# Two buffers in turn for the experts' scaled outputs, one buffer for the low part of their input

## The chip, the cores and the metric

The kernel runs on one core of a Trainium2 chip. The core has a matrix engine (TensorE, PE in the profile), a vector engine (DVE), a scalar engine (ACT), a general engine (POOL) and a queue engine (SP) that only issues transfers. Each engine runs its own instructions strictly in their order. Transfers between memory and the on-chip buffers run on 16 DMA engines, whichever engine issued them. The metric is the device time of one execution in microseconds, as the median of several runs.

## The reference

A trunk of two layers over 1024 tokens of width 1024, all in 32-bit floats. Each layer mixes the tokens (attention for one half of the width, a recurrent delta rule for the other), projects, and then sends every token to 2 of 32 experts. The change lies in the experts alone:

```python
def block_mlp(args):
    tok, e = args                      # up to 128 tokens of expert e
    xb = h_pad[tok]                    # gather, 128 x 1024
    hid = jax.nn.silu(xb @ w_gate[e]) * (xb @ w_up[e])     # 128 x 256
    return hid @ w_down[e]             # 128 x 1024
...
y = jax.ops.segment_sum(yb.reshape(R, D) * row_w[:, None], row_tok, num_segments=T + 1)
...
x = x + gt2 * hier_moe(...)
```

Each output row is scaled with the weight of its token for that expert, and by the gate `gt2`, before the two rows of a token are added.

## The kernel before

`layer` runs twice, once per layer. In each it runs `phase_a` (norm, input projection, attention, recurrence), `out_proj` (output projection and routing), and then `moe`, the stage of the experts. Nothing of the next layer starts before `moe` has written all rows, since the next norm reads them.

`moe` loops over 35 blocks of up to 128 tokens: the 32 experts and 3 blocks for rows beyond 128. The weights of a block come as two halves of 1 MB for gate and up (`w_gu`, `load_gu`, L1586) and 1 MB for down (`w_d`, `load_d`, L1589), issued on SP. Halves live in 5 slots (`self.raw`), so half n takes the slot of half n-5. Each half is split into a rounded part `w_hi` (ACT, L1594) and the rest `w_lo` (DVE, L1595), in 3 pairs of tiles (`self.parts`).

For a block e the steps are these:

- `gather(e)` (POOL, L1614): an indirect transfer fetches the rows of its tokens into `xg`, two tiles in turn.
- `prepare(e)`: 8 transposes on PE (L1622) into `xT_ps`, a rounded copy `xT_hi` on ACT (L1630), and the rest `xT_lo` on DVE (L1631).
- `up(e)`: 24 matmuls on PE, in threes: `xT_hi` with `w_hi` (L1646), `xT_lo` with `w_hi` (L1647), `xT_hi` with `w_lo` (L1648).
- `hidden(e)`: the activation, one step on ACT (L1636) and two on DVE (L1637, L1638), into `th`.
- `turned(e)`: two transposes of `th` on PE (L1666), copied to `hT` on ACT (L1667).
- `down(e)`: 4 matmuls on PE (L1687) into `y_ps`; the trace has two records for each.
- `scaled(e)`: DVE multiplies `y_ps` with the row weights and `gt2` into `yo` (L1673).
- `scatter(e)` (POOL, L1676): an indirect transfer writes the rows of `yo` to their places in `yd`.

The order on PE, ACT, DVE and POOL is fixed by the code (`in_order`). In turn e of the loop it is: up(e); the split of half 2e+3; turned(e-1); prepare(e+1); gather(e+3); hidden(e); down(e-1); scaled(e-1); scatter(e-1); the split of half 2e+4. So on DVE one turn reads: `w_lo` of half 2e+3, `xT_lo` of e+1, two steps of `th`, `yo` of e-1, `w_lo` of half 2e+4. The loads on SP, the routing of the extra rows (`route_overflow`, L1563 and L1564, in the first turns) and the rest of the kernel are put in order by a scheduler.

`yo` is one tile with one buffer (`tag="x", bufs=1` in the pool `tx`). The tile of block e+1 is the same memory, so its writer waits until the transfer of block e has read it. `xT_lo` has two buffers in the pool `xE`.

Of the kernel before, what the change touches and what calls it, by code (L numbers as in the profile page):

```python
# [10 lines left out]
F32 = mybir.dt.float32  # L11
F32R = mybir.dt.float32r
# [3 lines left out]
OP = mybir.AluOpType  # L16
# [4 lines left out]
T = 1024  # L21
D = 1024
# [30 lines left out]
class Trunk:  # L53
# [1546 lines left out]
    def moe(self, l, side, psum):  # L1600

        nc, tc = self.nc, self.tc
        with ExitStack() as s:
            xp, tx = s.enter_context(self.pool(name="xE", bufs=2, side=side)), self.tx
            gt2 = tx.tile([128, D], F32, name="gt2", tag="v2", bufs=1)
# [12 lines left out]
            def transposed(e):  # L1618
                x = xg[e % 2]
                pt = psum.tile([128, 8, 128], F32, name="xT_ps", tag="xT", bufs=1)  # L1620
                for k in range(NK):
                    nc.tensor.transpose(pt[:, k, :], x[:, 128 * k:128 * k + 128], self.ident)  # L1622
                return pt

            def prepare(e):

                pt = transposed(e)
                hi = tx.tile([128, 8, 128], F32R, name="xT_hi", tag="hl")
                lo = xp.tile([128, 8, 128], F32R, name="xT_lo", tag="xT_lo")
                nc.scalar.copy(hi, pt)  # L1630
                nc.vector.tensor_tensor(lo, pt, hi.bitcast(F32), op=OP.subtract)  # L1631
                return hi, lo
# [18 lines left out]
            def prepare_late(e):  # L1651
                pt = transposed(e)
                nc.scalar.copy(late, pt)
                return late
# [11 lines left out]
                    nc.tensor.transpose(pt[:, k, :], ths[:, e % 2, 128 * k:128 * k + 128], self.ident)  # L1666
                nc.scalar.copy(hT, pt)  # L1667

            yos = {}

            def scaled(e, po):
                yo = yos[e] = tx.tile([128, D], F32, name="yo", tag="x", bufs=1)
                nc.vector.scalar_tensor_tensor(yo, po, self.wsl[:, e:e + 1], gt2, op0=OP.mult, op1=OP.mult)  # L1673

            def scatter(e):
                st = nc.gpsimd.indirect_dma_start(out=self.yd, out_offset=bass.IndirectOffsetOnAxis(ap=self.idx_s[:, e:e + 1], axis=0),  # L1676
                                                  in_=yos.pop(e), in_offset=None, bounds_check=2 * T - 1, oob_is_err=False)
                for o in scat:
                    tc.declare_no_dep(st.ins, o.ins, reason="every slot holds another row")
                scat.append(st)  # L1680

            def down(e):
                w = self.wd[e % 3]
                po = psum.tile([128, D], F32, name="y_ps", tag="y", bufs=1)
                for half in range(2):
                    for k in range(2):
                        nc.tensor.matmul(po[:, 512 * half:512 * half + 512], hT[:, k, :], w[:, k, 512 * half:512 * half + 512],  # L1687
                                         start=(k == 0), stop=(k == 1))
                scaled(e, po)
# [16 lines left out]
            gather(0)  # L1706
            gather(1)
            x, last = prepare(0), {}
            gather(2)
            for e in range(N):  # L1710
                with self.in_order(last):
                    ph = up(e, x)
                    if e + 1 < N:
                        self.split_half(2 * e + 3)
                    if e:
                        turned(e - 1)
                    if e + 1 < N:
                        x = prepare(e + 1)
                    if e + 3 < N:
                        gather(e + 3)  # L1720
                    hidden(e, ph)
                if e == 0:
                    nc.sync.dma_start(gt2, self.mod_row(l, 5).partition_broadcast(128))
                with self.in_order(last):
                    if e:
                        down(e - 1)
                        scatter(e - 1)
                    if e + 2 < N:
                        self.split_half(2 * e + 4)
                for n in (2 * e + 8, 2 * e + 9):  # L1730
                    if n < 2 * N:
                        self.load_gu(l, n, expert(n // 2))
                if e and e + 2 < N:
                    self.load_d(l, e + 2, expert(e + 2))
                if e == 2:
                    self.route_overflow(xp, psum)
            turned(N - 1)
            down(N - 1)
            scatter(N - 1)
            late = self.lay.tile([128, 8, 128], F32, name="xT", tag="sg")  # L1740

            n = nc.values_load(self.ovf[0:1, 0:1], min_val=0, max_val=15)
            with ExitStack() as ifs:
                for b in range(self.MORE_E, 15):
                    ifs.enter_context(tc.If(n > b))
                    if b == self.MORE_E:
                        gather(32 + b)
                        overflow(b)
                    x = prepare_late(32 + b)
                    if b + 1 < 15:  # L1750
                        gather(33 + b)
                        overflow(b + 1)
                    up_late(32 + b, x)
                    turned(32 + b)
                    down(32 + b)
                    scatter(32 + b)
# [191 lines left out]
```

## Time and profile before

| | |
|---|---|
| median of 3 runs | 2877.4 us (2875.11 to 2880.29) |
| the profiled execution | 2878.6 us, of which the span from the first to the last instruction is 2876.6 us |
| PE busy | 2426.0 us, 84% of the span |
| DVE busy | 1862.8 us, 65% |
| ACT busy | 1108.6 us, 39% |
| POOL busy | 875.3 us, 30% |
| mean granted clock of PE | 0.904 of full speed |
| first to last copy of `hT`, layer 0 | 1038.2 to 1410.4 us |
| first to last copy of `hT`, layer 1 | 2430.4 to 2812.0 us |

The copy of `hT` (L1667) runs once per block at a fixed place in PE's order, so the distance of two such copies is the time of one block. The shares of busy time are means over stages with different limits; for a change in the experts the stretches 1038 to 1410 us and 2430 to 2812 us are to be read by themselves. A wait "<-X" is the idle time of an engine before an instruction, put down to what ended it.

### The profile page before, as it was taken

The numbers are of one execution on the slowest core, as the hardware profiler recorded it, in microseconds if no ns is written. First come the engines' busy times: TensorE is split into PE (matmuls) and PEld (weight loads), VectorE is DVE, ScalarE is ACT, GpSimd is POOL, SyncE is SP. The second block draws the span as 40 slices with busy tenths as digits, with TensorE's granted clock in tenths as the row PEclk, the third lists the DMA queues.
The fourth block names the chain that finished last, engine by engine and source line by source line (L and its number), as shares of the span: only waits on it lengthen the run. The fifth ranks groups of instructions, "written<-read, shape, count | busy, mean of one in ns | idle before, by whom it ended". The sixth has DMA issues, their size and how long they took to land.

```text
span 2876.6 us, 45429 instructions
## 1 busy us (share of the span) xinstructions
PE 2426.0 (84%) x17313; PEld 1847.9 (64%) x17313; DVE 1862.8 (65%) x3875; ACT 1108.6 (39%) x1988; POOL 875.3 (30%) x565
## 2 busy tenths in 40 slices
PE   5998997999789689998669878999878986988991
PEld 3766665777678666665447666777766775655660
DVE  5367775555684767666465787756567567656765
ACT  3333332343362244444243333334345332444541
POOL 4122232221420524444322212222232032334432
PEclk8999987998899789999889878889878986999996
DMA  8486674452532468888533333554444225888964
GB/s 285 152 256 208 198 228 127 134 151 88 187 103 89 162 237 312 318 321 326 196 126 109 108 103 124 167 149 125 119 150 125 88 110 177 324 300 299 330 247 187
DMA packets 262789, 542.70 MB, mean 189 GB/s; under 512 B 76376, under 2 KB 180768, under 8 KB 232608
## 3 DMA queue, kind: packets, MB, share of 16 engines
q1 hardware_dynamic: 234560, 484.61, 50.1%
q0 software_dynamic: 23376, 40.99, 3.9%
q10 hardware_dynamic: 4624, 14.06, 1.2%
q8 instruction: 142, 2.33, 0.3%
q14 instruction: 87, 0.71, 0.1%
HBM read 459.29 MB, written 120.09 MB: 201 GB/s over the span
## 4 chain that ended last, share of the span: by engine, by line
PE 40%; issue 20%; DVE 19%; DMA 10%; POOL 7%; ACT 3%; SPq 1%; POOLq 0%; DVEq 0%; ACTq 0%
PE pj L350 5%; PE pj L352 4%; PE pj L351 4%; POOL xg L1614 4%; POOL yd L1676 2%; DMA sp_z<-z 2%; DVE sv_t L741 2%; DVE sv_m L739 2%; PE po L1299 2%; PE at_o L1196 2%; PE po L1300 2%; PE po L1301 2%; DMA yd<-yo,idx_s 1%; DMA ada_w<-in_ada_w 1%; PE rb_y L899 1%
## 5 line engine op out<-in xcount | busy, mean ns | idle before, releaser
L1594 ACT CAST w_hi<-w_gu 128x2048 fp32r<-128x2048 f32 x140 | 266.8, 1907 | 283.8 <-PE h_ps L1647 279.7
L350 PE MATMUL pj<-hh,wa_hi 128*128 128x512 f32 x800 | 340.7, 426 | 2.4 <-ACT wa_hi L337 1.7
L351 PE MATMUL pj<-hl,wa_hi 128*128 128x512 f32 x800 | 331.3, 414 | 1.4 <-DVE hl L327 1.3
L352 PE MATMUL pj<-hh,wa_lo 128*128 128x512 f32 x800 | 327.5, 411 | 3.2 <-POOL wa_lo L338 3.2
L1676 POOL DMA_INDIRECT yd<-yo,idx_s x70 | 183.6, 2623 | 445.1 <-DVE yo L1673 425.6
L1595 DVE TENSOR_TENSOR w_lo<-w_gu,w_hi 128x2048 fp32r<-128x2048 f32 x134 | 301.6, 2284 | 20.2 <-ACT w_hi L1594 20.2
L1647 PE MATMUL h_ps<-w_hi,xT_lo 128*128 128x512 f32 x560 | 225.2, 402 | 54.7 <-DVE xT_lo L1631 54.6
L1687 PE MATMUL y_ps<-w_d,hT 128*128 128x512 f32 x560 | 254.3, 597 | 13.0 <-issue 5.8
L1673 DVE SCALAR_TENSOR_TENSOR yo<-y_ps,wsl,gt 128x1024 f32<-128x1024 f32 x70 | 89.9, 1284 | 237.5 <-DMA yd<-yo,idx_s 199.0
L1646 PE MATMUL h_ps<-w_hi,xT_hi 128*128 128x512 f32 x560 | 243.5, 435 | 0.0
L1648 PE MATMUL h_ps<-w_lo,xT_hi 128*128 128x512 f32 x560 | 220.2, 393 | 0.0
L338 POOL TENSOR_TENSOR wa_lo<-wa_raw,wa_hi 128x1024 fp32r<-128x1024 f32 x50 | 120.9, 2417 | 308.3 <-ACT wa_hi L337 237.4
L350 PEld LDWEIGHTS pj<-hh,wa_hi 128*128 128x128 f32 x800 | 157.7, 197 | 41.5 <-issue 6.0
L351 PEld LDWEIGHTS pj<-hl,wa_hi 128*128 128x128 f32 x800 | 157.2, 196 | 39.0 <-issue 5.2
L352 PEld LDWEIGHTS pj<-hh,wa_lo 128*128 128x128 f32 x800 | 156.9, 196 | 39.1 <-POOL wa_lo L338 4.4
L1687 PEld LDWEIGHTS y_ps<-w_d,hT 128*128 128x128 f32 x560 | 101.0, 190 | 117.3 <-issue 108.2
L1647 PEld LDWEIGHTS h_ps<-w_hi,xT_lo 128*128 128x128 f32 x560 | 105.8, 189 | 106.6 <-DVE xT_lo L1631 84.4
L1614 POOL DMA_INDIRECT xg<-h2d,idx_g x70 | 119.9, 1713 | 89.3 <-PE ro_pv L1564 49.7
L1646 PEld LDWEIGHTS h_ps<-w_hi,xT_hi 128*128 128x128 f32 x560 | 106.3, 190 | 33.3 <-issue 12.9
L1167 DVE TENSOR_REDUCE at_mx<-at_s 128x1 f32<-128x256 f32 (+7 forms) x128 | 95.9, 752 | 38.4 <-PE at_s L1165 37.5
L1648 PEld LDWEIGHTS h_ps<-w_lo,xT_hi 128*128 128x128 f32 x560 | 105.8, 189 | 20.5
L1169 ACT ACTIVATE at_p<-at_s,at_mx 128x256 f32<-128x256 f32 (+7 forms) x128 | 94.9, 743 | 62.3 <-DVE at_mx L1167 61.7
(435 smaller groups left out, 5389.8 us busy)
## 6 DMA issues: line engine op xcount, KB each, us to landing
w_gu<-in_moe_w_gu SPq DMA_DIRECT2D x140, 1024.0 KB
w_d<-in_moe_w_down SPq DMA_DIRECT2D x70, 1024.0 KB
ada_w<-in_ada_w SPq DMA_DIRECT2D x80, 512.0 KB
wa_raw<-in_w_in SPq DMA_DIRECT2D x50, 512.0 KB
sp_z<-z SPq DMA_DIRECT2D x32, 768.0 KB
b_zz<-sp_z SPq DMA_DIRECT2D x32, 512.0 KB
cy<-yd SPq DMA_DIRECT2D x16, 1024.0 KB
qkv<-qst SPq DMA_DIRECT2D x48, 256.0 KB
```

The source lines that it names most:

```text
L338: nc.gpsimd.tensor_tensor(lo, raw, hi.bitcast(F32), op=OP.subtract)
L350: nc.tensor.matmul(ps, hi[:, k, :], self.hh[k][:, sl], start=(k == 0), stop=False)
L351: nc.tensor.matmul(ps, hi[:, k, :], self.hl[k][:, sl], start=False, stop=False)
L352: nc.tensor.matmul(ps, lo[:, k, :], self.hh[k][:, sl], start=False, stop=(k == NK - 1))
L1594: self.nc.scalar.copy(hi, raw)
L1595: eng.tensor_tensor(lo, raw, hi.bitcast(F32), op=OP.subtract)
L1614: nc.gpsimd.indirect_dma_start(out=xg[e % 2], out_offset=None, in_=self.h2d, in_offset=bass.IndirectOffsetOnAxis(ap=self.idx_g[:, e:e + 1] ...
L1646: nc.tensor.matmul(ph, hi[:, k, :], whi[:, k % 4, :], start=(k == 0), stop=False)
L1647: nc.tensor.matmul(ph, lo[:, k, :], whi[:, k % 4, :], start=False, stop=False)
L1648: nc.tensor.matmul(ph, hi[:, k, :], wlo[:, k % 4, :], start=False, stop=(k == NK - 1))
L1676: st = nc.gpsimd.indirect_dma_start(out=self.yd, out_offset=bass.IndirectOffsetOnAxis(ap=self.idx_s[:, e:e + 1], axis=0), in_=yos.pop(e), ...
L1687: nc.tensor.matmul(po[:, 512 * half:512 * half + 512], hT[:, k, :], w[:, k, 512 * half:512 * half + 512], start=(k == 0), stop=(k == 1))
```

## The change

Two tiles for `yo` are made once, before the loop: one in the pool `tx` with its old tag, and one in the pool `xE`. Block e uses tile e modulo 2. To pay for the second, `xT_lo` gets one buffer in place of two; both are tiles of 4 KB per partition, so the memory in use is the same.

```diff
-                lo = xp.tile([128, 8, 128], F32R, name="xT_lo", tag="xT_lo")
+                lo = xp.tile([128, 8, 128], F32R, name="xT_lo", tag="xT_lo", bufs=1)
...
-            yos = {}
+            yos = [p.tile([128, D], F32, name="yo", tag="x", bufs=1) for p in (tx, xp)]
 
             def scaled(e, po):
-                yo = yos[e] = tx.tile([128, D], F32, name="yo", tag="x", bufs=1)
-                nc.vector.scalar_tensor_tensor(yo, po, self.wsl[:, e:e + 1], gt2, op0=OP.mult, op1=OP.mult)
+                nc.vector.scalar_tensor_tensor(yos[e % 2], po, self.wsl[:, e:e + 1], gt2, op0=OP.mult, op1=OP.mult)
 
             def scatter(e):
                 st = nc.gpsimd.indirect_dma_start(out=self.yd, out_offset=bass.IndirectOffsetOnAxis(ap=self.idx_s[:, e:e + 1], axis=0),
-                                                  in_=yos.pop(e), in_offset=None, bounds_check=2 * T - 1, oob_is_err=False)
+                                                  in_=yos[e % 2], in_offset=None, bounds_check=2 * T - 1, oob_is_err=False)
```

On DVE the order of the instructions in the loop stays as it is. What changes is what `yo` waits for. DMASW0 to DMASW7 are counters that the transfers issued by POOL use in turn; a gather and a scatter are issued per block, so a scatter's counter has a number two higher than the scatter's of the block before. Before, at two successive blocks of layer 0:

```order
L1673 SCALAR_TENSOR_TENSOR yo<-y_ps,wsl,gt_10476 128x1024 [waits DMASW3_49,PE_49]
L1595 TENSOR_TENSOR w_lo_10323<-w_gu_10329,w_hi_10322 128x2048 [waits DMAHW0_49,Activation_49]
L1595 TENSOR_TENSOR w_lo_10325<-w_gu_10330,w_hi_10324 128x2048 [waits DMAHW2_49,PE_49,Activation_49]
L1631 TENSOR_TENSOR xT_lo<-xT_ps,xT_hi 128x1024 [waits Activation_49]
L1637 SCALAR_TENSOR_TENSOR th<-th,h_ps 128x256 [waits Activation_49]
L1638 TENSOR_TENSOR th<-th,h_ps 128x256 [waits DVE_49]
L1673 SCALAR_TENSOR_TENSOR yo<-y_ps,wsl,gt_10476 128x1024 [waits DMASW5_49,PE_49]
```

The same place now:

```order
L1672 SCALAR_TENSOR_TENSOR yo<-y_ps,wsl,gt_10476 128x1024 [waits DMASW1_49,PE_49]
L1595 TENSOR_TENSOR w_lo_10323<-w_gu_10329,w_hi_10322 128x2048 [waits DMAHW0_49,Activation_49]
L1595 TENSOR_TENSOR w_lo_10325<-w_gu_10330,w_hi_10324 128x2048 [waits DMAHW2_49,PE_49,Activation_49]
L1631 TENSOR_TENSOR xT_lo<-xT_ps,xT_hi 128x1024 [waits Activation_49]
L1637 SCALAR_TENSOR_TENSOR th<-th,h_ps 128x256 [waits Activation_49]
L1638 TENSOR_TENSOR th<-th,h_ps 128x256 [waits DVE_49]
L1672 SCALAR_TENSOR_TENSOR yo<-y_ps,wsl,gt_10476 128x1024 [waits DMASW3_49,PE_49]
```

Each `yo` now waits for the scatter one block earlier than before, and `xT_lo`, with one buffer, waits for ACT alone as it did with two.

On SP the scheduler moved loads. In layer 0, about turn 8 of the loop, it read before (`w_gu` with a number is a slot of a half, `w_d` of a down matrix):

```order
L1586 DMA w_gu_10328<-in_moe_w_gu 128x2048
L1589 DMA w_d_9797<-in_moe_w_down 128x2048
L1586 DMA w_gu_10329<-in_moe_w_gu 128x2048
L1589 DMA w_d_10469<-in_moe_w_down 128x2048
L1586 DMA w_gu_10330<-in_moe_w_gu 128x2048
L1586 DMA w_gu_9795<-in_moe_w_gu 128x2048
L1589 DMA w_d_10470<-in_moe_w_down 128x2048
L1586 DMA w_gu_9796<-in_moe_w_gu 128x2048
```

It reads now:

```order
L1586 DMA w_gu_10328<-in_moe_w_gu 128x2048
L1589 DMA w_d_9797<-in_moe_w_down 128x2048
L1586 DMA w_gu_10329<-in_moe_w_gu 128x2048
L1586 DMA w_gu_10330<-in_moe_w_gu 128x2048
L1589 DMA w_d_10469<-in_moe_w_down 128x2048
L1586 DMA w_gu_9795<-in_moe_w_gu 128x2048
L1586 DMA w_gu_9796<-in_moe_w_gu 128x2048
L1589 DMA w_d_10470<-in_moe_w_down 128x2048
```

Up to turn 7 both have the first half of a turn, the load of `w_d`, the second half. Before, from turn 8 on, `w_d` stood first and both halves behind it; now the early pattern goes on to the last blocks, in both layers. Two more places are touched: one matmul of `route_overflow` moves by one block, and in the token mixing of layer 1 the scheduler swaps neighbouring pieces of work (138 of 6921 rows of PE's order, most of them in the recurrence).

## Rows read from the trace of the kernel before

**Rows 1.** Whole span: line, engine, operation xcount | busy us, mean ns | idle before <-releasers.

```profile
L1673 DVE SCALAR_TENSOR_TENSOR yo<-y_ps,wsl,gt 128x1024 f32<-128x1024 f32 x70 | 89.9, 1284 | 237.5 <-DMA yd<-yo,idx_s 199.0 <-PE hT_ps L1666 15.2 <-PE y_ps L1687 9.1
...
L1647 PE MATMUL h_ps<-w_hi,xT_lo 128*128 128x512 f32 x560 | 225.2, 402 | 54.7 <-DVE xT_lo L1631 54.6
...
L1594 ACT CAST w_hi<-w_gu 128x2048 fp32r<-128x2048 f32 x140 | 266.8, 1907 | 283.8 <-PE h_ps L1647 279.7
```

**Rows 2.** Line L1667, one window per layer: count, duration, first and last start in us.

```profile
L1667 ACT COPY hT<-hT_ps x35: 372/372/373, 1038.2 to 1410.4; 128x256 f32<-128x256 f32 x35
...
L1667 ACT COPY hT<-hT_ps x35: 372/372/374, 2430.4 to 2812.0; 128x256 f32<-128x256 f32 x35
```

**Rows 3.** Timeline of ACT: start, duration, line, operation [idle before <-releaser].

```profile
1048.66 0.37 ACT L1667 COPY hT<-hT_ps 128x256 f32<-128x256 f32 x1 [1.31 <-PE hT_ps L1666]
...
1059.10 0.37 ACT L1667 COPY hT<-hT_ps 128x256 f32<-128x256 f32 x1 [1.31 <-PE hT_ps L1666]
...
1158.30 0.37 ACT L1667 COPY hT<-hT_ps 128x256 f32<-128x256 f32 x1 [1.31 <-PE hT_ps L1666]
...
1168.32 0.37 ACT L1667 COPY hT<-hT_ps 128x256 f32<-128x256 f32 x1 [1.31 <-PE hT_ps L1666]
...
2807.53 0.37 ACT L1667 COPY hT<-hT_ps 128x256 f32<-128x256 f32 x1 [7.90 <-PE hT_ps L1666]
...
2811.97 0.37 ACT L1667 COPY hT<-hT_ps 128x256 f32<-128x256 f32 x1 [3.78 <-PE hT_ps L1666]
```

**Rows 4.** Timeline of all engines over one block that waits.

```profile
1167.12 1.28 DVE L1673 SCALAR_TENSOR_TENSOR yo<-y_ps,wsl,gt 128x1024 f32<-128x1024 f32 x1 [4.25 <-DMA yd<-yo,idx_s]
...
1168.32 4.48 DVE L1595 TENSOR_TENSOR w_lo<-w_gu,w_hi 128x2048 fp32r<-128x2048 f32 x2
...
1168.68 2.80 POOL L1676 DMA_INDIRECT yd<-yo,idx_s  x1 [6.84 <-DVE yo L1673]
...
1172.72 1.22 DVE L1631 TENSOR_TENSOR xT_lo<-xT_ps,xT_hi 128x1024 fp32r<-128x1024 f32 x1
...
1173.99 0.50 PE L1647 MATMUL h_ps<-w_hi,xT_lo 128*128 128x512 f32 x1 [1.22 <-DVE xT_lo L1631]
...
1179.45 1.28 DVE L1673 SCALAR_TENSOR_TENSOR yo<-y_ps,wsl,gt 128x1024 f32<-128x1024 f32 x1 [4.73 <-DMA yd<-yo,idx_s]
```

**Rows 5.** The same view over an early block of layer 0.

```profile
1050.66 1.90 ACT L1594 CAST w_hi<-w_gu 128x2048 fp32r<-128x2048 f32 x1
...
1053.13 1.28 DVE L1673 SCALAR_TENSOR_TENSOR yo<-y_ps,wsl,gt 128x1024 f32<-128x1024 f32 x1 [0.61 <-PE y_ps L1687]
...
1054.34 2.28 DVE L1595 TENSOR_TENSOR w_lo<-w_gu,w_hi 128x2048 fp32r<-128x2048 f32 x1
...
1060.96 1.22 DVE L1631 TENSOR_TENSOR xT_lo<-xT_ps,xT_hi 128x1024 fp32r<-128x1024 f32 x1 [0.55 <-ACT xT_hi L1630]
```

**Rows 6.** Stretches: length, busy PE, PEld, DVE, ACT, POOL; granted clock, DMA share, GB/s.

```profile
1048.66:1059.10 10.44, 10.44 (x49) 7.52 (x47) 8.24 (x9) 5.37 (x5) 3.81 (x2) 1.00 0.97 357
...
1091.30:1350.30 259.00, 236.00 (x969) 161.25 (x967) 173.91 (x143) 123.49 (x116) 106.19 (x46) 1.00 0.87 319
...
2430.40:2472.20 41.80, 41.80 (x186) 30.10 (x185) 31.43 (x31) 21.49 (x20) 14.22 (x8) 1.00 0.94 346
2440.87:2451.33 10.46, 10.46 (x49) 7.54 (x48) 8.26 (x9) 5.37 (x5) 3.82 (x2) 1.00 0.98 374
...
2494.20:2646.50 152.30, 125.60 (x506) 84.22 (x505) 91.74 (x74) 64.40 (x60) 56.59 (x25) 1.00 0.81 297
```

**Rows 7.** Tiles yo and xg, layer 0: indirect transfers from issue to landing, min/median/max us.

```profile
DMA to landing us min/median/max: 4.8/9.9/11.0
...
DMA to landing us min/median/max: 6.0/10.2/11.4
```

**Rows 8.** Line L672, the recurrence's first products, one window per layer, as Rows 2.

```profile
L672 PE MATMUL aa<-arv,bk x512: 268/270/473, 150.6 to 426.8; 64*64 64x128 f32 x171
...
L672 PE MATMUL aa<-arv,bk x512: 267/270/473, 1556.6 to 1840.4; 64*64 64x128 f32 x171
```

## The prediction

> **What bounds the kernel now.** I read the groups of instructions first. Two stand out in the experts' stage. DVE's `yo` idles 237.5 us over 70 blocks, 199.0 us of it ended by the scatter transfer of the block before; and PE idles 54.6 us ahead of the matmuls that read `xT_lo`, ended by DVE [rows 1]. The first costs something only if the second follows from it, so the timeline of one waiting block comes next [rows 4]. `yo` starts at 1167.12 after 4.25 us of waiting. Behind it on DVE stand two `w_lo` (4.48 us) and `xT_lo`, which starts at 1172.72; PE's second matmul of the next block starts at 1173.99, after 1.22 us of idling for it. So DVE's wait reaches PE. The scatter of this `yo` is issued at 1168.68, and the next `yo` waits for its landing till 1179.45: 12.33 us from `yo` to `yo`. That is a closed loop: 1.56 us from the start of `yo` to the issue, then the landing, whose median is 9.9 us [rows 7], is about 11.5 us a block, and no engine's speed comes into it.
>
> What would PE need? The copies of `hT` mark the blocks. Where nothing holds PE up, two successive copies stand 10.02 us apart (1158.30 to 1168.32), and 10.44 us in the first blocks, where routing work is mixed in (1048.66 to 1059.10) [rows 3]; PE is busy for all of that stretch at the full granted clock, 1.00, the 2.4 GHz level [rows 6]. In the first blocks the scatter lands in time, and the order of the loads is already the one that the change has throughout. An early block thus shows the changed kernel's rhythm: `yo` waits 0.61 us for `y_ps` of PE, `xT_lo` 0.55 us for ACT [rows 5]. DVE has slack; it works 8.24 us of 10.44 with routing pieces in it [rows 6].
>
> **The change part by part.** *The second `yo`.* The wait moves to the scatter two blocks back. `yo` starts every 10.02 us, so a scatter has 2 x 10.02 - 1.56 = 18.5 us to land; it takes 11.0 at most in layer 0 [rows 7]. The wait goes, and what is late next is PE's own order. Each layer has 35 copies of `hT`, hence 34 steps: 1038.2 to 1410.4 is 372.2 us, 2430.4 to 2812.0 is 381.6 us [rows 2]. At PE's pace: 5 steps with routing work at 10.45 are 52.3; 28 at 10.02 are 280.6; the last, with no next block, stays 4.4 (2807.53 to 2811.97) [rows 3]. Sum 337.3 us per layer. Saved: 34.9 + 44.3 = 79.2 us. What follows the last copy has the same work and stays.
>
> *One `xT_lo`.* Its writer must come after the last matmul of the block before that reads it. But it already reads `xT_ps`, whose transposes stand behind all those matmuls in PE's order, and its list of waits in the order is unchanged. Nothing is queued behind a new wait: 0 us. Were the cover gone, the wait would be some of the 0.55 us of slack at that place [rows 5].
>
> *The loads.* One half per turn is issued without waiting for the down product that frees `w_d`. This brings loads forward and costs no instruction. Yet the same megabytes must come in less time, and that has a price. Take the stretch of layer 1 with the longest steps, 2494.2 to 2646.5, 12 blocks: 297 GB/s x 152.3 us = 45.2 MB [rows 6]. At PE's pace there are 120.2 us for it. The highest rate held over four blocks is 346 GB/s, over one block 374 [rows 6]: 130.7 us or 120.9, a lag of 10.5 or 0.7 us. In layer 0, 1091.3 to 1350.3, 23 blocks: 82.6 MB, 238.8 us at 346 against 230.5, a lag of 8.3 or none. Against a lag stands the lead of the loads. A slot is free when its `w_lo` ends, 1056.62; the half cast at 1050.66 [rows 5] has a successor in that slot five halves later, two and a half blocks, about 1075.7. That is 19 us from issue to need. The trace gives no landing for these loads; the nearest rows are the indirect transfers beside them, up to 11.4 us [rows 7], so some 7 us of lead are free. It fits that ACT's casts now wait for PE and for no load (279.7 of 283.8 us) [rows 1]. The lag beyond the lead is 3.5 us in layer 1 and 1.3 in layer 0 at 346 GB/s, nothing at 374. I take 4 us, near the 346, since four blocks say more of a long stretch than one; the bounds are 0 and 5.
>
> The Trainium skill, HBM Reference, Specifications, gives a core about 358 GB/s as its share and says that a core streaming alone measures well above it, about 425. The 374 GB/s here agree with the second half. By 358 the lag in layer 1 would be an estimated 6 us, by 425 none; by either the 4 us would be 0, and the sum would be 4 us lower.
>
> *The swapped pieces in layer 1's mixing.* They have no row of their own. The nearest: the recurrence's products take 276.2 us in layer 0 and 283.8 in layer 1, the same work in two orders [rows 8]. I take 0, with 8 us either way.
>
> Sum: the profiled execution took 2878.6 us. 2878.6 - 79.2 + 4 = 2803.4. It lay 1.2 us above the median of 2877.4, so I forecast 2802 us, 2.6% faster.
>
> **The rivals.**
>
> *The transfers set the pace.* If the queues give on long stretches no more than the 319 GB/s of layer 0's waiting stretch [rows 6], 82.6 MB need the same 259 us as now, and the loads take over the wait from the scatter: no gain, about 2877. At 335 GB/s layer 1's stretch lags 14.7 us, 7.7 beyond the lead, and layer 0's 16.1, 9.1 beyond it: 2878.6 - 79.2 + 16.8 - 1.2 = 2815. Halfway between the two ends, 2845. For it: the DMA share is already 0.87 and 0.97 in the best stretch. Against it: 346 GB/s over 41.8 us at a PE that never paused, and 374 over one block.
>
> *The gathers become the bound, and the kernel is slower.* With two `xg` in turn, gather(e+3) is issued once the transposes of block e+1 are done and must land before those of e+3: it has somewhat less than two steps, 20.0 us. Beyond that a step is at least half of a landing. The 56 steps at PE's pace stand today at a mean of (372.2 + 381.6 - 104.6 - 8.8) / 56 = 11.43 us [rows 2, 3], so the kernel is slower from a landing of about 23 us; at 24 a step is 12.0 and the 56 steps cost 32 us more than now: 2909. For it: the gathers share the queues with loads that come denser, and the landings range from 6.0 to 11.4 us already [rows 7]. Against it: the longest would have to double.
>
> *The wait stays.* If the two tiles were released together, each `yo` would still wait for the scatter just before: 2877. Against it: the order names, for the second `yo` shown, the counter of two scatters back.
>
> **How the numbers follow.** Forecast 0.80; transfers set the pace 0.12 (0.09 of it with more than a 0.2% gain, 0.03 with none); the wait stays 0.02; gathers 0.03; slower by some other disturbance in the reordered mixing 0.03. So faster 0.89, same 0.05, slower 0.06; 0.2% is about what a measurement of this kernel can tell from no change. The forecast's own band: 4 us of lag may be 0 (2798) or 5 (2803), and the mixing adds 8 either way: 2790 to 2811. To leave out no more than 2 in 10 the range goes on into the case of the transfers, past the 335 GB/s case: 2789 to 2835.
>
> **What would show it.** In the changed profile the copies of `hT` should stand 10.02 us apart from the sixth block on, 337 us a layer; `yo` should wait under 1 us, and for PE; PE's waits for `xT_lo` should fall from 54.6 us to under 5; the stage should move about 350 GB/s. Steps over 10.3 us in 2500 to 2650 with ACT waiting for `w_gu` would show the transfers; PE waiting for `xg` before its transposes, the gathers; `xT_lo` waiting for PE, that one buffer is too few. A change of the time between 1410 and 2430 us other than an even shift would be the mixing. The forecast is wrong if the steps stay near 11.4 us, or if the mixing moves by more than 8 us.

## The result

The changed kernel takes 2795.46 us (median of 4 runs, 2792.54 to 2800.66) against 2876.26 us of the kernel before (4 runs, 2871.46 to 2880.29): a ratio of 0.9722, with a 95% interval of 0.9700 to 0.9743, so 2.8% faster. In a later comparison the same two gave 0.9706 (0.9687 to 0.9725).

The profiled execution of the changed kernel took 2794.4 us, with a span of 2792.5. The copies of `hT`, which [rows 2] show for before, now read (view of one tile, one window per layer: count, duration, first and last start):

```profile
L1667 ACT COPY hT<-hT_ps x35: 372/372/372, 1040.1 to 1377.6; 128x256 f32<-128x256 f32 x35
...
L1667 ACT COPY hT<-hT_ps x35: 372/372/373, 2391.7 to 2729.2; 128x256 f32<-128x256 f32 x35
```

From the first to the last copy it takes 337.5 us in either layer, instead of 372.2 and 381.6. So 34.7 + 44.1 = 78.8 us are gone from the experts. The rest of the span is the start to the first copy (1038.2 before, 1040.1 now), the stretch from the last copy of layer 0 to the first of layer 1 (1020.0 before, 1014.2 now) and what follows the last copy (64.6 before, 63.3 now): +1.9, -5.8 and -1.3. Together 2878.6 - 78.8 + 1.9 - 5.8 - 1.3 = 2794.6 us, against 2794.4 measured.

The timeline of the changed kernel in the place of [rows 4], ACT and DVE (start, duration, engine, line, operation, idle time before):

```profile
1162.70 0.37 ACT L1667 COPY hT<-hT_ps 128x256 f32<-128x256 f32 x1 [1.31 <-PE hT_ps L1666]
...
1172.72 0.37 ACT L1667 COPY hT<-hT_ps 128x256 f32<-128x256 f32 x1 [1.31 <-PE hT_ps L1666]
...
1166.95 1.28 DVE L1672 SCALAR_TENSOR_TENSOR yo<-y_ps,wsl,gt 128x1024 f32<-128x1024 f32 x1 [0.39 <-PE y_ps L1686]
1168.16 2.28 DVE L1595 TENSOR_TENSOR w_lo<-w_gu,w_hi 128x2048 fp32r<-128x2048 f32 x1
1171.44 2.29 DVE L1595 TENSOR_TENSOR w_lo<-w_gu,w_hi 128x2048 fp32r<-128x2048 f32 x1 [1.01 <-ACT w_hi L1594]
1174.58 1.22 DVE L1631 TENSOR_TENSOR xT_lo<-xT_ps,xT_hi 128x1024 fp32r<-128x1024 f32 x1 [0.85 <-ACT xT_hi L1630]
...
1176.97 1.28 DVE L1672 SCALAR_TENSOR_TENSOR yo<-y_ps,wsl,gt 128x1024 f32<-128x1024 f32 x1 [0.39 <-PE y_ps L1686]
```

The copies and the `yo` both come 10.02 us apart. `yo` waits 0.39 us, and for PE; the 4 us for the scatter are gone. The slack now lies with DVE, which idles 1.01 and 0.85 us for ACT, and ACT in turn waits for PE.

The view of the tile `yo` over the whole span (idle time by what ended it, with the number of times), and its transfers from issue to landing:

```profile
  PE y_ps L1686: 41.0, 70
...
DMA to landing us min/median/max: 2.5/10.0/11.9
```

All 70 `yo` wait for PE, 0.59 us in the mean, and none for a transfer. The scatters land as late as before (a median of 10.0 us, and 9.9 in [rows 7]), but no `yo` waits for them.

The groups that answer to [rows 1] (busy us, mean ns, idle before, releaser), with the two indirect transfers on POOL:

```profile
L1594 ACT CAST w_hi<-w_gu 128x2048 fp32r<-128x2048 f32 x140 | 266.9, 1908 | 209.8 <-PE h_ps L1647 203.0
...
L1675 POOL DMA_INDIRECT yd<-yo,idx_s x70 | 183.6, 2622 | 293.2 <-DVE yo L1672 278.5
...
L1647 PE MATMUL h_ps<-w_hi,xT_lo 128*128 128x512 f32 x560 | 222.9, 398 | 1.4 <-DVE xT_lo L1631 1.4
...
L1614 POOL DMA_INDIRECT xg<-h2d,idx_g x70 | 71.7, 1024 | 214.1 <-PE xT_ps L1622 126.6
```

PE's wait for `xT_lo` has gone from 54.6 us to 1.4. And the stretches that answer to [rows 6] (length, busy PE, PEld, DVE, ACT, POOL; granted clock, DMA share, GB/s), 23 blocks of each layer:

```profile
1098.60:1328.90 230.30, 230.30 (x967) 162.49 (x966) 178.03 (x139) 123.57 (x115) 86.11 (x47) 1.00 0.97 361
2450.30:2680.60 230.30, 230.30 (x967) 162.48 (x966) 178.03 (x139) 123.57 (x115) 87.47 (x47) 1.00 0.98 361
```

PE is busy for the whole of both, at the full granted clock (2.4 GHz), and the transfers run at 361 GB/s where they ran at 319 and 297.

### The profile page after: what moved, and what is told of

Read it like the earlier page. It is cut to its first block, busy times and chain, and to the rows that moved or that the text cites. A ratio compares the mean times of both kernels' runs of the same rounds, so it can differ in the third digit from the quotient of the medians.

```text
span 2792.5 us, 45428 instructions
## 1 busy us (share of the span) xinstructions
PE 2407.7 (86%) x17313; PEld 1847.2 (66%) x17313; DVE 1869.9 (67%) x3875; ACT 1109.7 (40%) x1988; POOL 830.8 (30%) x565
## 3 DMA queue, kind: packets, MB, share of 16 engines
q0 software_dynamic: 23376, 40.99, 4.0%
## 4 chain that ended last, share of the span: by engine, by line
PE 43%; DVE 18%; issue 15%; DMA 10%; POOL 8%; ACT 3%; SPq 1%; POOLq 0%; DVEq 0%; ACTq 0%
POOL yd L1675 5%; PE pj L350 5%; PE pj L352 5%; PE pj L351 5%; DMA sp_z<-z 2%; PE at_o L1196 2%; POOL xg L1614 2%; DVE sv_m L739 2%; DVE sv_t L741 2%; PE po L1299 2%; DMA ada_w<-in_ada_w 2%; PE po L1300 2%; PE po L1301 2%; DMA yd<-yo,idx_s 1%; PE y_ps L1686 1%
## 5 line engine op out<-in xcount | busy, mean ns | idle before, releaser
L1614 POOL DMA_INDIRECT xg<-h2d,idx_g x70 | 71.7, 1024 | 214.1 <-PE xT_ps L1622 126.6
L1631 DVE TENSOR_TENSOR xT_lo<-xT_ps,xT_hi 128x1024 fp32r<-128x1024 f32 x70 | 85.7, 1224 | 51.8 <-ACT xT_hi L1630 51.8
L1167 DVE TENSOR_REDUCE at_mx<-at_s 128x1 f32<-128x256 f32 (+7 forms) x128 | 95.8, 753 | 35.4 <-PE at_s L1165 34.7
```

Of the source, the lines that this page charges most:

```text
L1614: nc.gpsimd.indirect_dma_start(out=xg[e % 2], out_offset=None, in_=self.h2d, in_offset=bass.IndirectOffsetOnAxis(ap=self.idx_g[:, e:e + 1] ...
```

## The experiments

Two theories stood against each other at first. **The loop**: a single `yo` ties each block to the issue and landing of the scatter before it, and the second tile alone brings the gain. **Everything else that moved**: the one buffer of `xT_lo`, the order of the loads, or the place of the tiles in memory brings part of it, or costs part of it. A third question came from the prediction's own 4 us: how near are the transfers to being the bound?

### One part alone: one buffer for `xT_lo`, still one `yo`

```diff
-                lo = xp.tile([128, 8, 128], F32R, name="xT_lo", tag="xT_lo")
+                lo = xp.tile([128, 8, 128], F32R, name="xT_lo", tag="xT_lo", bufs=1)
```

> The kernel before, with one buffer for xT_lo and still one yo; its instructions stand in the order of before on every engine. Theory (the gain is the second yo alone, one xT_lo costs nothing, because its writer already waits for transposes that stand behind all readers of the old tile): the time of before, 2876 us within 0.2%, and hT to hT 372 and 382 us. Rival (one xT_lo buffer costs something that the second yo hides): slower, by up to 70 waits of 0.55 us, 38 us. Rival (one xT_lo brings part of the gain): faster by over 6 us.

Measured: a median of 2883.3 us against 2874.6, a ratio of 1.0022 (1.0001 to 1.0042). Its copies of `hT` and its `yo`:

```profile
L1667 ACT COPY hT<-hT_ps x35: 372/373/374, 1040.8 to 1431.7; 128x256 f32<-128x256 f32 x35
...
L1667 ACT COPY hT<-hT_ps x35: 372/373/374, 2447.5 to 2827.5; 128x256 f32<-128x256 f32 x35
...
L1673 DVE SCALAR_TENSOR_TENSOR yo<-y_ps,wsl,gt 128x1024 f32<-128x1024 f32 x70 | 89.9, 1284 | 256.5 <-DMA yd<-yo,idx_s 233.8
```

No part of the gain comes from this line. Layer 1 takes 379.9 us, as before; layer 0 takes 390.9, 18.7 more than in the one profiled execution of before, with more waiting for scatters (233.8 us against 199.0) and no wait of `xT_lo` for PE. The profiled execution was the longest of the twelve, 2894.1 us. The instructions and their order are those of before. Whether the 0.2% is a cost of this edit, or chance in a stage that hangs on how late each scatter lands, stays open; a way in which one buffer would cost it was not seen.

### The second tile is there, but not used

```diff
-                nc.vector.scalar_tensor_tensor(yos[e % 2], po, ...)
+                nc.vector.scalar_tensor_tensor(yos[0], po, ...)
...
-                                                  in_=yos[e % 2], ...)
+                                                  in_=yos[0], ...)
```

> The changed kernel with its two yo tiles in memory, but every block uses the first of them. Theory (the wait of yo for the scatter of the block before is all): back to the time of before, 2876 us within 0.3%, yo idle some 200 us for DMA, and the loads in the order of before, since the scheduler chose the new order because of the second tile. Rival (the gain comes from where the tiles lie, or from one xT_lo): stays near 2795.

Measured: 2878.1 us, ratio 1.0009 (0.9987 to 1.0031). The whole gain is gone:

```profile
L1667 ACT COPY hT<-hT_ps x35: 372/372/373, 1050.8 to 1425.8; 128x256 f32<-128x256 f32 x35
...
L1667 ACT COPY hT<-hT_ps x35: 372/372/373, 2439.9 to 2810.7; 128x256 f32<-128x256 f32 x35
...
L1672 DVE SCALAR_TENSOR_TENSOR yo<-y_ps,wsl,gt 128x1024 f32<-128x1024 f32 x70 | 89.9, 1284 | 231.0 <-DMA yd<-yo,idx_s 212.9
```

375.0 and 370.8 us, and the wait for the scatter is back, 212.9 us. The order of the loads is that of before again, so this run does not tell it from the wait; a later one does. Neither the place of the tiles nor the one buffer of `xT_lo` is behind the gain.

### The changed kernel with two buffers for `xT_lo`

```diff
-                lo = xp.tile([128, 8, 128], F32R, name="xT_lo", tag="xT_lo", bufs=1)
+                lo = xp.tile([128, 8, 128], F32R, name="xT_lo", tag="xT_lo")
```

> The changed kernel with two buffers for xT_lo again (4 KB more per partition); its instructions stand in the order of the changed kernel on every engine. Theory (one buffer costs nothing): 2795 us within 0.2%, 337.5 us from the first to the last hT in both layers. Rival (one buffer costs a little in each block): faster by up to 70 x 0.1 us = 7 us or more, with steps under 10.02 us.

Measured: 2797.4 us, ratio to before 0.9724 (0.9697 to 0.9751), where the changed kernel has 0.9722.

```profile
L1667 ACT COPY hT<-hT_ps x35: 372/373/373, 1041.7 to 1379.2; 128x256 f32<-128x256 f32 x35
```

337.5 us again, and 337.5 in layer 1. With two `yo` the second buffer of `xT_lo` is worth nothing, as the prediction had it. It also shows that the memory for both was there, so that the `xT_lo` part of the change was not needed.

### The loads in the order of before

From turn 8 to turn 27, `w_d` is put ahead of both halves in SP's queue:

```diff
+                if 8 <= e < 28:
+                    with self.in_order(queued, (nc.sync,)):
+                        self.load_d(l, e + 2, e + 2)
+                        for n in (2 * e + 8, 2 * e + 9):
+                            self.load_gu(l, n, n // 2)
...
```

> The changed kernel with the loads on SP held in the order of before from turn 8 on (w_d first, behind the down product that frees its slot, then both halves). Theory (the second yo is all, the loads have lead enough in either order): hT to hT stays 337.5 us in both layers, total 2795 to 2802 (2801 if the mixing of layer 1 takes the order of before, some 6 us longer). Rival (the earlier loads bring part of the gain): steps over 10.2 us in the blocks from the eighth on, and ACT waiting for w_gu; if all of it, 2876.

Measured: 2789.0 us, ratio 0.9705 (0.9677 to 0.9733).

```profile
L1667 ACT COPY hT<-hT_ps x35: 372/372/373, 1033.3 to 1370.7; 128x256 f32<-128x256 f32 x35
...
L1667 ACT COPY hT<-hT_ps x35: 372/372/373, 2377.9 to 2715.4; 128x256 f32<-128x256 f32 x35
```

337.5 us in both layers. The earlier loads bring nothing; their new order on SP was no part of the gain.

### The loop made longer, with one `yo` and with two

A copy of `yo` on POOL delays every scatter; it is added once to the kernel before and once to the changed one.

```diff
+            junk = xp.tile([128, D], F32, name="junk", tag="junk", bufs=1)
...
             def scatter(e):
+                nc.gpsimd.tensor_copy(junk, yos[e])
                 st = nc.gpsimd.indirect_dma_start(out=self.yd, ...
```

> The kernel before (one yo), with a copy of yo to an unused tile on POOL ahead of every scatter, which issues the scatter X later, X about 1 to 2.5 us by the trace of this run. Theory (the loop from yo over the scatter's issue and landing to the next yo paces the stage): the mean step grows by nearly X, from 10.95 and 11.22 us to 10.95 + X and 11.22 + X in the two layers, since nearly all steps are then at the loop's pace; with X of 2 us the kernel takes some 2876 + 68 x 2 = 3010 us. Rival (the order of the loads, or the transfers, pace the stage; POOL is idle 70% of the time): 2876 as before, within 1%.

> The same copy on POOL in the changed kernel (two yo). Theory (a scatter then has 2 x 10.02 - 1.56 - X = 16 us or more to land, and lands in 11.9 at most): steps stay at 10.02 us and 337.5 us a layer, total about 2795, unless the copy on POOL slows DVE so far that PE waits for it. Rival (POOL's own work or its share of memory ports is near the bound): steps over 10.2 us.

Measured: 3057.6 us with one `yo` (ratio 1.0627, 1.0555 to 1.0700) and 2794.7 us with two (0.9714, 0.9662 to 0.9765). The copy and the `hT` of the kernel with one:

```profile
L1677 POOL COPY junk<-yo 128x1024 f32<-128x1024 f32 x70 | 200.0, 2857 | 493.9 <-DVE yo L1674 486.6
...
L1668 ACT COPY hT<-hT_ps x35: 372/373/374, 1043.3 to 1523.4; 128x256 f32<-128x256 f32 x35
...
L1668 ACT COPY hT<-hT_ps x35: 372/373/374, 2517.6 to 2995.5; 128x256 f32<-128x256 f32 x35
```

The same rows of the kernel with two:

```profile
L1676 POOL COPY junk<-yo 128x1024 f32<-128x1024 f32 x70 | 196.3, 2804 | 208.5 <-DVE yo L1673 202.5
...
L1668 ACT COPY hT<-hT_ps x35: 372/372/373, 1038.8 to 1376.3; 128x256 f32<-128x256 f32 x35
```

With one `yo` the layers take 480.1 and 477.9 us, 107.9 and 96.3 more: over 34 steps 3.17 and 2.83 us a step, for a copy of 2.86. The expectation had put X at up to 2.5 us and 3010 us for an X of 2; by the measured X it would be 2876 + 68 x 2.86 = 3070. With two `yo` the same 2.8 us cost nothing: 337.5 us, although POOL is busier there, 161.73 of 230.30 us in the 23 blocks from 1098.60, against 173.11 of 381.40 us from 1098.60 on with one. With one `yo`, PE is busy 293.29 us of that stretch, at a mean granted clock of 0.92; but the `yo` wait 371.4 us for the scatter in all, 61 times, so the loop and not PE sets the steps. So it is the length of the loop that counts with one tile, not how busy any engine is, and the second tile opens the loop. This is the plainest proof of the theory here.

### Why the scatter takes 10 us: fewer loads beside it

The kernel before, one `yo`, without the loads of `w_d` from the fourth expert on.

```diff
-        self.nc.sync.dma_start(self.wd[i % 3], self.expert_source(l, e, "moe_w_down"))
+        if i < 3 or i >= 32:
+            self.nc.sync.dma_start(self.wd[i % 3], self.expert_source(l, e, "moe_w_down"))
```

> The kernel before (one yo) without the loads of w_d from the fourth expert on: old weights are used, 1 MB less comes in per block. Theory (the scatter itself is short; it lands late because its rows stand among the loads' packets on the same 16 DMA engines): its landing falls from about 10 us to under 8, the loop of 1.56 us plus the landing falls below PE's 10.02, steps of 10.02 us, 337.5 us a layer, total about 2797 with a single yo. Rival (the scatter takes its 10 us by its own length): steps stay at 10.9 to 11.2 us, total 2876.

Measured: 2785.5 us, ratio 0.9696 (0.9670 to 0.9723). The copies of `hT`, the `yo`, PE's wait, and the landing of the scatters:

```profile
L1668 ACT COPY hT<-hT_ps x35: 372/372/373, 1039.9 to 1383.9; 128x256 f32<-128x256 f32 x35
...
L1674 DVE SCALAR_TENSOR_TENSOR yo<-y_ps,wsl,gt 128x1024 f32<-128x1024 f32 x70 | 89.9, 1284 | 129.3 <-DMA yd<-yo,idx_s 115.2
...
L1648 PE MATMUL h_ps<-w_hi,xT_lo 128*128 128x512 f32 x560 | 223.1, 398 | 8.7 <-DVE xT_lo L1632 8.6
...
DMA to landing us min/median/max: 2.5/8.5/12.0
```

The landing fell from 9.9 to 8.5 us, not below 8 as expected, and that is enough: 344.0 us in layer 0 and 343.6 in layer 1 with a single `yo`. In layer 0 the steps are those of the changed kernel up to the 25th, and only the next seven are longer, up to 12.40 us. `yo` still waits 115.2 us, 50 times, but PE only 8.6: a wait of some 2 us a block drowns in DVE's slack, and the one of 3.75 (199.0 over 53 in the kernel before) did not. Of the 94 us that this kernel gains, 66 are in the experts; 29.5 are in the stretch between the layers, which is 990.5 us long here (see below).

So the traffic beside the scatter lengthens its landing, by 1.4 us in the median for the 1 MB per block that is gone here; what makes up the other 8.5 us this run does not show. In the changed kernel the shortest landing, 2.5 us, is among the last blocks of layer 1, where the loads run out; the median there is 5.1 us, and 10.1 over the blocks ahead of it. But those last blocks hold few rows (the last section has the number), so they do not show what the traffic alone does.

### How much room the transfers have

Half a MB more to load per block, in the changed kernel:

```diff
+            spare = xp.tile([128, 1024], F32, name="spare", tag="spare", bufs=1)
...
                 if e and e + 2 < N:
                     self.load_d(l, e + 2, expert(e + 2))
+                    if e + 2 < 32:
+                        nc.sync.dma_start(spare, self.expert_source(l, e + 2, "moe_w_down")[:, 0, :])
```

> The changed kernel with half a MB more to load per block from the second block to the 30th (half of w_d once more, to an unused tile). Theory (the transfers lie just below PE's pace): 4.0 to 4.3 MB per block need 10.8 to 11.5 us at 372 GB/s, steps of about 11 us there, PE waiting for weights, total about 2795 + 2 x 28 x 1.0 = 2850 us, 2825 to 2880. Rival (room in the queues as at 411 GB/s in one block of the changed kernel): steps of 10.02 to 10.3 us, total under 2812.

Measured: 2794.4 us, ratio 0.9713 (0.9661 to 0.9764): no cost. The copies of `hT`, ACT's waits, and the stretches as above:

```profile
L1668 ACT COPY hT<-hT_ps x35: 358/372/373, 1038.1 to 1383.7; 128x256 f32<-128x256 f32 x35
...
L1668 ACT COPY hT<-hT_ps x35: 359/372/374, 2389.0 to 2727.8; 128x256 f32<-128x256 f32 x35
...
L1594 ACT CAST w_hi<-w_gu 128x2048 fp32r<-128x2048 f32 x140 | 266.7, 1906 | 262.1 <-DMA w_gu<-in_moe_w_gu 145.7
...
1098.60:1328.90 230.30, 225.02 (x943) 158.22 (x942) 169.56 (x133) 117.64 (x112) 98.07 (x45) 1.00 0.98 383
2450.30:2680.60 230.30, 229.94 (x962) 161.66 (x961) 176.98 (x138) 121.67 (x116) 95.21 (x46) 1.00 0.99 389
```

345.6 and 338.8 us: 8.1 and 1.3 us more in all, where the expectation had some 28 in each. (A stretch between the layers that was 1005.3 us long hides it in the total.) ACT now waits 145.7 us for weights, so the transfers begin to be felt: in layer 0 at 383 GB/s, with PE busy 225.02 of 230.30 us. Layer 1 carried 389 GB/s with PE busy 229.94 us, so there 389 is what was asked for and not a limit. The expectation had taken 372 GB/s for the ceiling, by dividing the rate of the changed kernel by its DMA share; that is refuted, for a share of 0.98 carried 383 here and 361 there.

The other side: less work for PE at the same traffic. The third matmul of `up` is left out, and with it that part of the product.

```diff
                     nc.tensor.matmul(ph, hi[:, k, :], whi[:, k % 4, :], start=(k == 0), stop=False)
-                    nc.tensor.matmul(ph, lo[:, k, :], whi[:, k % 4, :], start=False, stop=False)
-                    nc.tensor.matmul(ph, hi[:, k, :], wlo[:, k % 4, :], start=False, stop=(k == NK - 1))
+                    nc.tensor.matmul(ph, lo[:, k, :], whi[:, k % 4, :], start=False, stop=(k == NK - 1))
```

> The changed kernel without the third matmul of up (xT_hi with w_lo), which leaves that part of the product out; loads, casts, w_lo on DVE, gathers and scatters stay. PE then needs some 8 x 0.21 = 1.7 us less per block, about 8.3 us. Theory (PE alone paces the changed kernel, and the transfers lie just below it, at a share of 0.97): steps fall, but only to what the transfers give, 3.4 to 3.8 MB per block at 361 GB/s / 0.97 = 372 GB/s, so 9.1 to 10.2 us, with ACT now waiting for w_gu. Rival (the transfers had room): steps of 8.3 us, or at DVE's 8 us. Rival (the transfers already pace it): steps stay at 10.02.

Measured: 2724.8 us, ratio 0.9471 (0.9385 to 0.9557).

```profile
L1666 ACT COPY hT<-hT_ps x35: 355/367/375, 1032.7 to 1345.0; 128x256 f32<-128x256 f32 x35
...
L1594 ACT CAST w_hi<-w_gu 128x2048 fp32r<-128x2048 f32 x140 | 266.8, 1907 | 257.3 <-DMA w_gu<-in_moe_w_gu 152.1
...
1085.00:1300.00 215.00, 193.65 (x759) 126.48 (x758) 170.38 (x137) 118.49 (x113) 97.00 (x45) 0.98 0.99 379
2410.00:2610.00 200.00, 179.28 (x718) 118.57 (x717) 159.69 (x127) 108.73 (x105) 91.09 (x43) 0.99 0.99 385
```

312.3 us in layer 0 and 307.9 in layer 1. Steps are 8.21 us where loads lie ready, in the first and the last blocks, and up to 10.9 between, with ACT waiting for weights: here the loads pace the stage, at 379 to 385 GB/s and a share of 0.99. So the loads of this stage come at 379 to 389 GB/s at best in the two runs, 5 to 8% above the 361 that the changed kernel asks for. Whether the transfers themselves or the five slots set this is not shown: between 1085 and 1300 us SP's loads of halves wait 147.8 us for a slot that a `w_lo` frees, and no run had more slots.

### A version with less work for PE

If PE paces the changed kernel and the loads leave a few per cent, less work on PE must pay. Half of the down product is made of three rounded matmuls in place of one in full precision:

```diff
+            def split_d(e):
+                raw = self.wd[e % 3][:, 0, :]
+                nc.scalar.copy(wd_hi, raw)
+                nc.gpsimd.tensor_tensor(wd_lo, raw, wd_hi.bitcast(F32), op=OP.subtract)
...
+                    for c in cols:
+                        nc.tensor.matmul(po[:, c], hT[:, 1, :], w[:, 1, c], start=True, stop=False)
+                    for i, (x, y) in enumerate(((hT_hi, wd_hi), (hT_lo, wd_hi), (hT_hi, wd_lo))):
+                        for c in cols:
+                            nc.tensor.matmul(po[:, c], x, y[:, c], start=False, stop=(i == 2))
```

> The changed kernel with less work for PE: the half of the down product that reads the first 128 rows of w_d is made of three rounded matmuls (as in up) in place of one in full precision; ACT rounds that half of w_d, POOL makes the rest ahead of the scatter, DVE a small rest of hT, and xT_hi has one buffer too. PE's down product takes 4 x 0.43 + 6 x 0.23 = 3.1 us in place of 3.43, so 0.35 us less per block. Theory (PE's order paces the changed kernel, the transfers leave room down to about 9.6 us): steps of about 9.67 us, 66 x 0.35 = 23 us less, total 2772 us; up to 2785 if the transfers hold some steps, as they held steps at 9.6 us on average when PE needed 8.21. Rival (ACT's, DVE's or POOL's added work comes late to PE): 2795 or more.

> The changed kernel once more, on the chip of the run beside it: 2795 us, 337.5 us from the first to the last hT in both layers; what differs between its runs lies outside the experts.

Measured: 2764.1 us, ratio to before 0.9604 (0.9585 to 0.9622); the changed kernel beside it 2792.5 us, 0.9706 (0.9687 to 0.9725). So this version beats both, by 1.0% the changed one. Its copies of `hT` (now of half the width), `w_lo` over the whole span, and two stretches:

```profile
L1675 ACT COPY hT<-hT_ps x35: 258/265/267, 1045.3 to 1370.4; 128x128 f32<-128x128 f32 x35
...
L1595 DVE TENSOR_TENSOR w_lo<-w_gu,w_hi 128x2048 fp32r<-128x2048 f32 x134 | 424.1, 3196 | 18.5 <-ACT w_hi L1594 18.5
...
1106.00:1340.00 234.00, 234.00 (x1067) 180.13 (x1066) 233.16 (x171) 155.52 (x173) 172.46 (x74) 1.00 0.97 371
2443.80:2675.00 231.20, 231.20 (x1056) 178.36 (x1055) 230.36 (x169) 153.15 (x168) 170.72 (x73) 1.00 0.97 371
```

325.1 us in both layers, 12.4 less each, 24.8 together for an expected 23. Steps are 9.64 us, PE's own time again. But DVE is now busy 233.16 of 234.00 us, with a mean `w_lo` of 3.20 us against 2.29: by these rows the next cut on PE would find DVE in its place, which no run tried.

## Why the prediction was right, and where it was off

It gave 2802 us (2789 to 2835) and 0.89 for faster; 2795.5 was measured.

- **The wait that goes, and what comes late next.** Right, to the step. 337.3 us per layer were worked out and 337.5 measured; 79.2 us saved and 78.8 measured. Copies stand 10.02 us apart; the one that differs from the sum is the sixth step, 10.22. That PE's own order is next was read from the few blocks of before in which nothing held PE up [rows 3, 5]. The two runs with the copy on POOL show the loop itself: 2.86 us more in it cost 2.83 to 3.17 us a step with one `yo` and nothing with two.
- **The loop, "no engine's speed comes into it".** This reading was too strong, though no term of the sum hangs on it. The landing is counted from the start of POOL's issue, and the issue of the block in [rows 4] took 2.80 us where the shortest took 0.97, because it waited for DVE's `w_lo` (last section). So about 1.8 of the 11.5 us are DVE's. Without them the loop is an estimated 9.7 us, less than PE's 10.02: `w_lo` at another place on DVE might have brought the gain, or most of it, with one tile. No run tried that.
- **One `xT_lo` costs nothing.** Right: PE waits 1.4 us for it in all, and a second buffer changes nothing.
- **The lag of the loads, +4 us.** This term was mis-sized: it is 0. The failed step is the choice of 346 GB/s as what the transfers can hold, because "four blocks say more of a long stretch than one". Those four blocks ran at PE's pace [rows 6]; the 346 was what they asked for, not a limit. The two runs on the transfers carried 379 to 389 GB/s over 200 us and more, above even the 374 that the prediction had at hand and did not take. Its sentence on the Trainium skill (HBM Reference, Specifications) holds: by 425 there is no lag, and none was measured; the 361 GB/s of the changed kernel and the 379 to 389 of the two runs lie above the 358 of a core's share.
- **The order of the loads** costs and brings nothing: with the order of before the layers take 337.5 us as well.
- **The swapped pieces in layer 1's mixing, 0 with 8 us either way.** The stretch between the layers is 5.8 us shorter, within the band, and the order is not needed to explain it. The kernel that leaves its second `yo` unused has the order of before, and its stretch is as short as that of the changed kernel, 1014.1 us against 1014.2 (1015.3 in the other profiled execution of the changed kernel). With the order of before it differs by 5.9 us between two kernels; the granted clock differs with it.

The stretch between the layers in the kernel before (columns as in [rows 6]):

```profile
1410.40:2430.41 1020.01, 842.51 (x6465) 673.03 (x6466) 666.05 (x1650) 372.21 (x819) 276.07 (x187) 0.86 0.40 127
```

In the kernel whose second `yo` is not used:

```profile
1425.80:2439.90 1014.10, 832.28 (x6466) 663.30 (x6467) 664.39 (x1650) 372.02 (x819) 278.70 (x187) 0.87 0.40 128
```

In the changed kernel:

```profile
1377.55:2391.75 1014.20, 834.29 (x6467) 665.05 (x6468) 667.24 (x1651) 372.91 (x819) 280.12 (x187) 0.87 0.41 129
```

And in the kernel without the loads of `w_d`:

```profile
1383.90:2374.40 990.50, 824.15 (x6465) 656.93 (x6466) 660.61 (x1650) 372.23 (x818) 275.84 (x187) 0.88 0.41 132
```

Over these the mean granted clock goes from 0.86 to 0.88 while the stretch goes from 1020.0 to 990.5 us.

- **The rivals.** That transfers set the pace is refuted for this kernel, but not far off: by the rates of 361 against 379 to 389 GB/s, an estimated 5 to 7% less PE time brings the loads in. At 9.64 us a step, 3.8% less, they were not in yet. That the gathers become the bound is refuted: PE waits for `xg` once per layer, ahead of the first block (5.3 and 5.2 us), and then the copies keep 10.02 us. That the wait stays is refuted by 41.0 us of waiting, all of it for PE.

For the profiled execution the steps gave 2803.4 us and 2794.4 were measured. Of these 9.0 us the lag is 4 and the stretch between the layers 5.8; the start (+1.9), the end (-1.3) and the experts (79.2 against 78.8) nearly cancel.

## What to carry to other kernels

A buffer that is written, sent off and written again is a loop of its own, whatever the engines have to do; add issue and landing, and compare the sum with the pace of the busiest engine before giving it a second buffer. Where a wait comes and goes, the blocks without it show the pace that the cure will bring. And a transfer rate read where an engine sets the pace is a demand: the ceiling has to be measured, by asking for more.

## What the runs showed of the hardware that was not expected

**POOL's issue of an indirect transfer waits for DVE.** The timeline of POOL and DVE over one block of the changed kernel:

```profile
2510.19 2.79 POOL L1675 DMA_INDIRECT yd<-yo,idx_s  x1 [3.75 <-DVE yo L1672]
2515.45 1.01 POOL L1614 DMA_INDIRECT xg<-h2d,idx_g  x1 [2.46 <-PE xT_ps L1622]
...
2509.83 2.28 DVE L1595 TENSOR_TENSOR w_lo<-w_gu,w_hi 128x2048 fp32r<-128x2048 f32 x1
```

`w_lo` ended at 2512.11. The scatter, issued beside it, ended at 2512.98, 0.87 us later, and took 2.79 us where the shortest in the trace took 0.97. The same holds for all 64 scatters of the changed kernel that met a `w_lo`: each ended 0.86 to 0.90 us after it. The gather met no `w_lo` and took 1.01. In the kernel before, a gather that was issued right behind the scatter met the second `w_lo` of [rows 4], which ended at 1172.80:

```profile
1171.78 1.91 POOL L1614 DMA_INDIRECT xg<-h2d,idx_g  x1 [0.30 <-issue]
```

It took 1.91 us and ended 0.89 us after that `w_lo`; so the mean of the gathers fell from 1.71 to 1.02 us with the change. The same holds the other way round, in the version with the split down product:

```profile
2516.14 2.39 POOL L1668 TENSOR_TENSOR wd_lo<-w_d,wd_hi 128x1024 fp32r<-128x1024 f32 x1 [2.03 <-ACT wd_hi L1667]
...
2516.45 4.22 DVE L1595 TENSOR_TENSOR w_lo<-w_gu,w_hi 128x2048 fp32r<-128x2048 f32 x1
```

Here `w_lo` took 4.22 us in place of 2.28, and ended 2.14 us after POOL's `wd_lo`. That is why DVE reads as full in that version: part of its busy time is waiting for POOL. The Trainium skill, SBUF — State Buffer, SBUF: two separate sides, states that DVE and GpSimd share a pair of ports as a lock held for a whole instruction, and that a DVE operation with two inputs from SBUF takes part only against a GpSimd operation that reads SBUF. The rows of `wd_lo`, which reads two tiles there, agree; those of the scatter and the gather show that the issue of an indirect transfer is held up by `w_lo` as well.

**The landing of a scatter hangs on the loads beside it, and its size is not that of its tile.** In the median a scatter lands in 8.5 us in the kernel whose experts move 247 to 258 GB/s, in 10.0 at 361, and in 10.1, hardly later, at 383 to 389. The landings of 2.5 us do not continue this row. A tile of `yo` is half a MB, but a scatter writes only the rows that its block holds: 2048 rows of 4 KB in a layer, over 35 blocks, are an estimated 0.24 MB in the mean. (The queue of the transfers that POOL issues moved 40.99 MB in the whole execution, where 140 full tiles would be 73.) For the scatter that landed in 2.54 us, issued at 2720.61 in the changed kernel, the stretch from issue to landing reads (columns as in [rows 6]):

```profile
2720.61:2723.15 2.54, 2.54 (x13) 2.10 (x12) 0.00 (x0) 0.00 (x0) 0.98 (x1) 1.00 0.08 23
```

23 GB/s over 2.54 us are 0.06 MB for all transfers together. So this scatter was short as well as alone, and what a full one takes with no load beside it is not shown.
